# Two-step token sums in the feed-forward, and head halves joined by engine writes across partitions

## The chip, the core and the metric

The kernel runs on one core of one Trainium2 chip. The metric is the device time of one launch, in microseconds (us). The core has a matrix engine (TensorE, PE in the profile, with its weight loads as PEld), a vector engine (DVE), a scalar engine (ACT), GpSimd (POOL) and SyncE (SP), whose queue issues the DMAs. Each engine works through its own instructions in order.

## What is computed

A stack of three blocks on 512 tokens of width 1024, in float32. The first block has forget-gate attention (FOX, 8 heads of 64) and latent attention (MLA, 8 heads of 64), each with a gate. It is followed by two equal layers, each with four mixers (A: a chunkwise mLSTM, B: grouped attention, C: neighbourhood attention, D: differential attention), a gated merge, and a feed-forward part of width 2816. What the change touches is, cut from the reference:

```python
fox = _block_sweep(fq, fk, fv, ...).reshape(B, L, FOX_WIDTH) * jax.nn.silu(f_gate)
mla = _block_sweep(q, k, mv, ...).reshape(B, L, MLA_WIDTH) * jax.nn.silu(m_gate)
o = jnp.einsum('bgrqk,bkgd->bqgrd', softmax(q @ k), v)      # B; C likewise with its own keys
ffn = (jax.nn.silu(h2 @ w_ffn_gate) * (h2 @ w_ffn_up)) @ w_ffn_down
```

## The kernel before

**Precision.** Every float32 operand of a product is split into a high and a low part. A weight block is split by `split_w`: ACT writes `whi` (L221), then POOL, or DVE for every `k.lo`-th block, writes `wlo` (L223). Three matmuls follow for one product (L250 to L252). `evict_split` does the same for results in PSUM: ACT copies the high part (L211), DVE subtracts it for the low part (L212).

**What sets the order.** Only PE's order is written out by hand (`manual_schedule`). The instructions of ACT, DVE, POOL and SP are ordered at build time by the framework, with a model of time, from the order in which the code emits them and from the tile buffers that are free. A tile pool has a fixed number of buffers per tag: `t2` has 6, `yn` (`gate_tile`) has 3, `A` (the PSUM banks) has 8, `qs` and `ks` have 2.

**Heads.** FOX, MLA, B and C keep each head's output in one PSUM bank of 128 partitions by 512 tokens (`Head`). Partitions 0 to 63 hold the product with the high part of the values, 64 to 127 that with the low part, and the output is their sum. B and C run in both layers, so there are 48 heads in 24 pairs. `Head.pv` closes a head at `t == 3` by an ACT copy of the whole bank to a `t2` tile `z` (L458). For every second head `pair_out` takes a third `t2` tile `e`, has SP copy the upper half of the first head's `z` to the lower half of `e`, and the lower half of the second head's `z` to the upper half of `e`, by two DMAs (L464, L465), and has DVE add the halves that already stand on the right partitions (L466, L467). The first head of a pair thus ends in `e[0:64]`, the second in `e[64:128]`. The pair's output is then gated and split (L1027, L1073, or the `out` of B and C).

**Around a head.** `overlap` writes out PE's order map by map: scores, transposes, products with the values and the end of a head, at fixed lags, with pieces of other work (`stream`) between. DVE works meanwhile on softmax (L342, L345, L1019), on the low parts of the probabilities (L212, tile `ptl`) that the next products (L455) wait for, and on evictions of the streamed work.

**Feed-forward.** `ffn` runs once per layer. The first two gate blocks and the first two up blocks are plain (`plain`, 24 products of 512 columns each); the other 20 and 20 blocks are taken two by two in `fast_pair`, which needs 7 products of half size instead of 8. For it DVE adds and subtracts quarters of the raw weights (L599 to L602), ACT and DVE split each sum (L591, L592), and PE multiplies it with token quarters or with sums of them. `Tokens.sums` makes these four token sums once per layer, in two steps over the feature slices `c`. A step is four subtractions on DVE (L571 to L574) into four `t2` tiles, and for each a high part by ACT (L576) and a low part by DVE (L577): 8 DVE and 4 ACT instructions. The token quarters that it reads lie in two `qs` and two `cst` tiles; the two `qs` tiles are afterwards reused for weights of the fast pairs. The first sum is used by the third product of the first fast pair.

The plain part reads:

```python
gts, us = [k.silu2(plain(gw), k.t2()) for _ in range(2)], []
tok.sums()
for _ in range(2):
    us.append(plain(uw))
```

`silu2` is a tanh by ACT (L365) into a `t2` tile and a multiplication by DVE (L366). `pair` then multiplies gate and up (L1193) and splits the result (L1195, L1196).

Of the kernel before, what the change touches and what calls it, by code (L numbers as in the profile page):

```python
# [14 lines left out]
ALU = mybir.AluOpType  # L15
# [3 lines left out]
P = 128  # L19
# [146 lines left out]
def hybrid_kernel(ctx: ExitStack, tc: tile.TileContext, i: dict, out: bass.AP):  # L166
    nc = tc.nc
    V, A_, G, T_ = nc.vector, nc.scalar, nc.gpsimd, nc.tensor
# [8 lines left out]
    k = Work()  # L177
# [6 lines left out]
    def bank():  # L184
        return new(ps_, [P, 512], "A", bufs=8)

    def f(ap):
        return ap.bitcast(F32)
# [129 lines left out]
    def t2(dt=F32):  # L318
        return new(pool, [P, 512], "t2", dt, 6)
# [88 lines left out]
    class Head:  # L408

        def __init__(self, v, blocks, meta=None):
            self.v, self.blocks, self.meta, self.pt, self.pm = v, blocks, meta, {}, {}

        def trans(self, t, p, col):

# [20 lines left out]
        def pv(self, t):  # L438

            if t % 2 == 0:  # L440
                return
            if t == 1:
                self.ps = bank()
            first, second = self.blocks(t - 1), self.blocks(t)
            ph, pl = self.pt[t // 2]
            parts = [(self.meta[0], *self.pm[t // 2], 0, 256)] if self.meta else []
            for b in sorted(set(first) | set(second), key=lambda b: not (b in first and b in second)):
                lo, hi = (0 if b in first else P), (256 if b in second else P)
                parts.append((self.v(b), ph[:, b], pl[:, b], lo, hi))
            o = (t // 2) * 256  # L450
            for j, (v, ph, pl, lo, hi) in enumerate(parts):
                last = j == len(parts) - 1
                passes = [(v, ph, P), (v[:, 0:64], pl, 64)]
                for w, q, m in (passes[::-1] if last else passes):
                    T_.matmul(self.ps[0:m, o + lo:o + hi], w, q[:, lo:hi], start=(j == 0 and m == P), stop=(last and m == P))  # L455
            if t == 3:
                self.z = t2()
                A_.copy(self.z, self.ps)  # L458

    def pair_out(heads):  # L460

        a, b = (h.z for h in heads)
        e = t2()
        nc.sync.dma_start(e[0:64], a[64:128])  # L464
        nc.sync.dma_start(e[64:128], b[0:64])  # L465
        V.tensor_tensor(e[0:64], a[0:64], e[0:64], ALU.add)  # L466
        V.tensor_tensor(e[64:128], b[64:128], e[64:128], ALU.add)  # L467
        return e

    def split_y(y, hi, lo):  # L470
        A_.copy(hi, y)
# [85 lines left out]
    class Tokens:  # L557
# [5 lines left out]
        def sums(self):  # L563

            (b11, b12), (b21, b22) = self.q
            hi = new(pool, [P, 4, 4, 256], "v", F32R, 1)
            lo = [new(pool, [P, 2, 4, 256], "ks", F32R) for _ in range(2)]
            self.t = [(hi[:, j], lo[j // 2][:, j % 2]) for j in range(4)]
            for c in (slice(0, 2), slice(2, 4)):
                t = [t2().rearrange("p (k c) -> p k c", k=2) for _ in range(4)]  # L570
                V.tensor_tensor(t[0], b12[:, c], b11[:, c], ALU.subtract)  # L571
                V.tensor_tensor(t[1], b22[:, c], t[0], ALU.subtract)
                V.tensor_tensor(t[2], b22[:, c], b12[:, c], ALU.subtract)
                V.tensor_tensor(t[3], b21[:, c], t[1], ALU.subtract)  # L574
                for j in (1, 2, 0, 3):
                    A_.copy(self.t[j][0][:, c], t[j])  # L576
                    V.tensor_tensor(self.t[j][1][:, c], t[j], f(self.t[j][0][:, c]), ALU.subtract)  # L577

        def quarter(self, a, b):
            return tuple(z[:, 4 * a:4 * a + 4, 256 * b:256 * b + 256] for z in self.h)  # L580
# [90 lines left out]
    with tc.manual_schedule(engines={mybir.EngineType.PE}):  # L671
        x, spill, h = first_block(k)
        with tc.tile_pool(name="mix", bufs=1) as mix:
            k.mix = mix
            for layer in range(N_LAYERS):
                spill, h = hybrid_layer(k, spill, h, layer, layer == N_LAYERS - 1)
# [51 lines left out]
def first_body(k, fb, col, hl):  # L728
    nc, i, new, f, pool, small, bank, stream = k.nc, k.i, k.new, k.f, k.pool, k.small, k.bank, k.stream
    V, A_, G, T_ = k.V, k.A_, k.G, k.T_  # L730
    w_in, h = i["w_in"], k.tokens(hl)
# [101 lines left out]
    qw, kw, gw = (k.w_cols(i["t_" + n]) for n in ("fq", "fk", "fg"))  # L833
# [40 lines left out]
    fox = Work()  # L874
# [9 lines left out]
    mla = Work()  # L884
# [120 lines left out]
    def fox_head(hd):  # L1005
        u, e = fox.units[hd // 2], hd % 2
        st = Work()
        hobj = head(hd, *fox.v)
        fox.heads[hd] = hobj

        def sc(t):
            if t == 0:
                st.cb = new(pool, [P, L], "cb")
                nc.sync.dma_start(st.cb, fox.rows[hd].partition_broadcast(P))
            sps, n = scores(t, [(u.qs[:, e, t * P:(t + 1) * P], u.ks[:, 2 * e + b]) for b in range(2)], k.mcr)
            p = k.p_tile(n)

            r = k.softmax_of_sum([(sp, st.cb[:, a:b], a, b) for sp, a, b in sps], p)[1]
            V.tensor_scalar(p, p, r, None, ALU.mult)  # L1019
            if t == 3 and hd in (1, 3):  # L1020
                v = fox.units[hd // 2 + 2]
                v.task = stream.push(fox_unit(v), U_COST, soon=True)
            return p

        def done():
            e = k.pair_out([fox.heads[hd - 1], fox.heads[hd]])
            V.scalar_tensor_tensor(e, e, 0.5, u.gate, ALU.mult, ALU.mult)  # L1027
            y1[hd // 2] = k.y_tile()
            k.split_y(e, *y1[hd // 2])

        return [maps_of(hd, t, sc, hobj, done if t == 3 and hd % 2 else None, u) for t in range(NT)]
# [15 lines left out]
    def mla_head(hd):  # L1047
        u = mla.units[hd]
        hobj = head(hd, *mla.v)
        mla.heads[hd] = hobj  # L1050

        def sc(t):
            sl = slice(t * P, (t + 1) * P)
            (qh, ql), (kh, kl) = u.q, u.k
            sps, n = scores(t, [(qh[:, sl], kh), (qh[:, sl], kl), (ql[:, sl], kh)], k.mkr)
            p = k.p_tile(n)
            r = k.softmax_banks(sps, p)
            if t % 2:
                A_.activation(p, p, AF.Copy, bias=0.0, scale=r)
            else:  # L1060
                V.tensor_scalar(p, p, r, None, ALU.mult)
            if t == 3 and hd < 6:

                v = mla.units[hd + 2]
                v.task = stream.push(mla_unit(hd + 2, v), 1100)
                if hd % 2 == 0:
                    gate(hd // 2 + 1)
            return p

        def done():  # L1070
            j = hd // 2
            e = k.pair_out([mla.heads[hd - 1], mla.heads[hd]])
            V.scalar_tensor_tensor(e, e, 0.5, gates[j], ALU.mult, ALU.mult)  # L1073
            if j >= 2:
                q = k.q_stack()
                y2.append((q[:, 0, 0:S], q[:, 1, 0:S]))
            k.split_y(e, *y2[j])

        return [maps_of(hd, t, sc, hobj, done if t == 3 and hd % 2 else None, u, q1) for t in range(NT)]
# [68 lines left out]
def ffn(k, x, l, h, quarters, last):  # L1148
    nc, i, new, V, A_, f, pool, bank, stream = k.nc, k.i, k.new, k.V, k.A_, k.f, k.pool, k.bank, k.stream
    gw, uw = (k.w_cols(i[n][l], lambda: new(pool, [P, 2 * L], "qs")[:, 0:1024]) for n in ("t_gate", "t_up"))  # L1150
    tok = k.Tokens(h, quarters)
# [6 lines left out]
    def plain(w):  # L1158
        ps = bank()
        for _ in k.proj_t([(ps, get)], next(w), KD):  # L1160
            pass
        return ps
# [16 lines left out]
    def pair(first):  # L1179

        if first:

            k.lo = 2
            gts, us = [k.silu2(plain(gw), k.t2()) for _ in range(2)], []
            tok.sums()
            for _ in range(2):
                us.append(plain(uw))
            k.lo = 1
        else:
            gts, us = [k.silu2(g, g) for g in fast(gw)], fast(uw)  # L1190
        out = []
        for u, gt in zip(us, gts):
            V.scalar_tensor_tensor(gt, u, 0.5, gt, ALU.mult, ALU.mult)  # L1193
            hi, lo = y_tiles()
            A_.copy(hi, gt)  # L1195
            V.tensor_tensor(lo, gt, f(hi), ALU.subtract)  # L1196
            out.append((hi, lo))
        return out
# [342 lines left out]
def pair_maps(k, j, head, score, out, unit=None, before=None):  # L1541

    heads = [head(2 * j + e) for e in range(2)]

    def one(e, t):
        st = Work()

        def sc():
            st.p, st.col = score(e, t)

        def done():
            out(k.pair_out(heads))

        needs = []
        if unit and e == 0 and t == 0:
            needs.append((0, lambda: unit.task))
        if before and e == 1 and t == 3:
            needs.append((3, lambda: before))
        return (sc, lambda: heads[e].trans(t, st.p, st.col), (lambda: heads[e].pv(t)) if t % 2 else None,
                done if e == 1 and t == 3 else None, needs)  # L1560

    return [one(e, t) for e in range(2) for t in range(NT)]
# [437 lines left out]
```

## Time and profile before

| | |
|---|---|
| three runs | 2560.34, 2564.12 (median), 2567.02 us |
| the profiled execution | 2570.03 us, of it 2568.2 us from the first to the last instruction |
| PE busy | 2488.4 us (97%) |
| DVE, ACT, POOL busy | 1602.7, 1329.6, 939.0 us (62%, 52%, 37%) |
| mean granted TensorE clock | 0.99 of 2.4 GHz |
| first feed-forward, plain part and first fast pair | about 1098 to 1142 us |
| second feed-forward, the same | about 2206 to 2251 us |

PE is busy nearly throughout. Time of the other engines matters where PE waits for it, so the profile is read from PE's waits: the list of who waited for whom, and the timeline around the longest of them.

### The profile page before, as it was taken

The page shows a single profiled execution, that of the slowest core. Times are in us where ns is not written, and L with a number is a line of the kernel's source. Part 1 is how long each engine was busy: PE and PEld are TensorE (multiplying, and loading weights), DVE is VectorE, ACT ScalarE, POOL GpSimd, SP SyncE. Part 2 cuts the span into 40 slices and gives each one's busy share as a digit, 9 for nine tenths or more (in the row PEclk, how much of TensorE's full clock was granted, in tenths as well). Part 3 has the DMA queues.
Part 4 walks back from the last instruction along what each step waited for, and adds up shares of the span by engine and source line. Part 5 has one row for each costly group of instructions (what it writes and reads, how often), then busy time and mean ns, then how long its engine had stood idle before and what let it go on. Part 6 is the DMA issues. An engine that isn't in the chain of part 4 may idle for free. (4 is left out here: it accounts for less than half of the span.)

```text
span 2568.2 us, 39912 instructions
## 1 busy us (share of the span) xinstructions
PE 2488.4 (97%) x14358; PEld 2159.6 (84%) x14358; DVE 1602.7 (62%) x3521; ACT 1329.6 (52%) x2893; POOL 939.0 (37%) x834
## 2 busy tenths in 40 slices
PE   7999999999999999989999999999999999899998
PEld 7988788888888878779999888888878878799997
DVE  3577557769335354577888567584354464787886
ACT  4567646647445444354444467475354453554443
POOL 4453346542565544400000456424655534100002
PEclk9999999999999999999999999999999999999999
DMA  5552233221537332422333232214374334232232
GB/s 149 145 142 68 88 128 103 77 95 55 145 105 189 106 105 83 148 91 99 101 106 107 99 110 88 88 57 132 108 186 115 97 89 135 87 107 99 101 105 82
DMA packets 117750, 277.20 MB, mean 108 GB/s; under 512 B 15824, under 2 KB 37584, under 8 KB 117552
## 3 DMA queue, kind: packets, MB, share of 16 engines
q1 hardware_dynamic: 117552, 274.65, 35.4%
q8 instruction: 113, 1.85, 0.3%
q14 instruction: 85, 0.70, 0.1%
HBM read 230.26 MB, written 6.46 MB: 92 GB/s over the span
## 5 line engine op out<-in xcount | busy, mean ns | idle before, releaser
L223 POOL TENSOR_TENSOR wlo<-raw,whi 128x512 fp32r<-128x512 f32 (+4 forms) x481 | 617.4, 1286 | 622.9 <-ACT whi L221 598.8
L221 ACT CAST whi<-raw 128x512 fp32r<-128x512 f32 (+4 forms) x573 | 345.7, 605 | 513.5 <-PE A L251 331.8
L250 PE MATMUL A<-hi,whi 128*128 128x512 f32 (+2 forms) x1368 | 535.5, 391 | 0.7 <-ACT hi L211 0.7
L252 PE MATMUL A<-hi,wlo 128*128 128x512 f32 (+2 forms) x1368 | 515.5, 377 | 2.7 <-POOL wlo L223 2.7
L251 PE MATMUL A<-lo,whi 128*128 128x512 f32 (+2 forms) x1368 | 516.8, 378 | 0.1
L252 PEld LDWEIGHTS A<-hi,wlo 128*128 128x128 f32 x1368 | 258.4, 189 | 53.8 <-POOL wlo L223 3.5
L250 PEld LDWEIGHTS A<-hi,whi 128*128 128x128 f32 x1368 | 258.7, 189 | 37.9 <-ACT hi L211 0.8
L251 PEld LDWEIGHTS A<-lo,whi 128*128 128x128 f32 x1368 | 259.1, 189 | 37.1 <-DVE lo L212 0.3
L651 POOL TENSOR_TENSOR ptl<-raw,pth 128x512 fp32r<-128x512 f32 x20 | 26.0, 1320 | 605.7 <-ACT pth L650 605.7
L212 DVE TENSOR_TENSOR ptl<-A,pth 128x512 fp32r<-128x512 f32 (+3 forms) x256 | 148.9, 582 | 103.9 <-ACT pth L211 102.5
L316 PE MATMUL A<-ident,p 128*128 128x128 f32 (+3 forms) x1125 | 176.2, 279 | 22.9 <-DVE p L540 17.5
L250 PE MATMUL A<-v,whi 128*128 128x256 f32 x640 | 182.3, 285 | 10.7 <-ACT whi L591 10.7
L316 PEld LDWEIGHTS A<-ident,p 128*128 128x128 f32 (+3 forms) x1125 | 136.5, 140 | 62.1 <-DVE p L540 19.7
L252 PE MATMUL A<-v,wlo 128*128 128x256 f32 x640 | 181.9, 284 | 3.8 <-DVE wlo L592 3.8
L251 PE MATMUL A<-ks,whi 128*128 128x256 f32 x640 | 181.2, 283 | 0.0
L344 ACT ACTIVATE p<-p,sms 128x512 f32<-128x512 f32 (+6 forms) x160 | 100.6, 629 | 121.0 <-DVE sms L342 116.1
L211 ACT CAST pth<-A 128x512 fp32r<-128x512 f32 (+3 forms) x256 | 128.0, 500 | 65.8 <-PE A L316 64.3
L223 DVE TENSOR_TENSOR wlo<-raw,whi 128x512 fp32r<-128x512 f32 x92 | 67.0, 728 | 125.4 <-ACT whi L221 125.2
L298 PE MATMUL A<-whi,hi 128*128 128x256 f32 (+7 forms) x440 | 144.5, 328 | 0.0
L300 PE MATMUL A<-whi,lo 128*128 128x256 f32 (+7 forms) x440 | 141.7, 322 | 0.0
L299 PE MATMUL A<-wlo,hi 128*128 128x256 f32 (+7 forms) x440 | 141.6, 322 | 0.0
L250 PEld LDWEIGHTS A<-v,whi 128*128 128x128 f32 x640 | 122.4, 191 | 17.2 <-ACT whi L591 11.2
(433 smaller groups left out, 6172.7 us busy)
## 6 DMA issues: line engine op xcount, KB each, us to landing
raw<-in_t_gl_dram SPq DMA_DIRECT2D x64, 512.0 KB, 3.5
raw<-in_w_ffn_down_dram SPq DMA_DIRECT2D x44, 512.0 KB, 3.6
raw<-in_w_in_dram SPq DMA_DIRECT2D x26, 512.0 KB, 3.5
raw<-in_w_out_dram SPq DMA_DIRECT2D x24, 512.0 KB, 3.6
raw<-in_t_gate_dram SPq DMA_DIRECT2D x24, 512.0 KB, 3.6
raw<-in_t_up_dram SPq DMA_DIRECT2D x24, 512.0 KB, 3.5
qs<-in_t_gate_dram SPq DMA_DIRECT2D x20, 512.0 KB, 4.4
qs<-in_t_up_dram SPq DMA_DIRECT2D x20, 512.0 KB, 4.2
```

The source lines that it names most:

```text
L211: A_.copy(hi, ps)
L212: V.tensor_tensor(lo, ps, f(hi), ALU.subtract)
L221: A_.copy(hi, src)
L223: (V if k.lo and k.turn % k.lo == 0 else G).tensor_tensor(lo, src, f(hi), ALU.subtract)
L250: T_.matmul(ps, sh, mh, start=first, stop=False, **kw)
L251: T_.matmul(ps, sh, ml, start=False, stop=False, **kw)
L252: T_.matmul(ps, sl, mh, start=False, stop=last, **kw)
L298: T_.matmul(ps, sh, wh[:, j], start=(b + j == 0), stop=False)
L299: T_.matmul(ps, sh, wl[:, j], start=False, stop=False)
L300: T_.matmul(ps, sl, wh[:, j], start=False, stop=(b + j == nk - 1))
L316: T_.transpose(dst, src, ident[0:k, 0:k])
L344: A_.activation(dst, dst, AF.Exp, bias=st[:, e:e + 1], scale=-1.0, accum_out=st[:, 2:3])
```

## The change

- `Head` gets a `mate`, the first head of its pair (none for a first head). At `t == 3` a first head takes the tile `e`, a second head takes its mate's. ACT copies one half of the bank (64 partitions) to the other 64 partitions of `e`: 64-127 to 0-63 for a first head, 0-63 to 64-127 for a second. DVE then adds the half of the bank that stands on the right partitions, from PSUM. `pair_out`, with its two DMAs and two additions, is gone, as are the two `z` tiles.
- `Tokens.sums` becomes a generator that stops after each step. The first step is emitted behind the first plain gate block, the second behind the second. The results of these two gate blocks go to `gate_tile()` (`yn`) instead of `t2`.

```diff
@@ Head.__init__ @@
-            self.v, self.blocks, self.meta, self.pt, self.pm = v, blocks, meta, {}, {}
+            self.v, self.blocks, self.meta, self.pt, self.pm, self.mate = v, blocks, meta, {}, {}, None
@@ Head.pv @@
             if t == 3:
-                self.z = t2()
-                A_.copy(self.z, self.ps)
-
-    def pair_out(heads):
-
-        a, b = (h.z for h in heads)
-        e = t2()
-        nc.sync.dma_start(e[0:64], a[64:128])
-        nc.sync.dma_start(e[64:128], b[0:64])
-        V.tensor_tensor(e[0:64], a[0:64], e[0:64], ALU.add)
-        V.tensor_tensor(e[64:128], b[64:128], e[64:128], ALU.add)
-        return e
+                self.e = self.mate.e if self.mate else t2()
+                own, other = (slice(64, P), slice(0, 64)) if self.mate else (slice(0, 64), slice(64, P))
+                A_.copy(self.e[own], self.ps[other])
+                V.tensor_tensor(self.e[own], self.ps[own], self.e[own], ALU.add)
@@ Tokens.sums, at the end of the loop over c @@
+                yield
@@ fox_head @@
+        hobj.mate = fox.heads[hd - 1] if e else None
-            e = k.pair_out([fox.heads[hd - 1], fox.heads[hd]])
+            e = hobj.e
@@ mla_head @@
+        hobj.mate = mla.heads[hd - 1] if hd % 2 else None
-            e = k.pair_out([mla.heads[hd - 1], mla.heads[hd]])
+            e = hobj.e
@@ ffn, pair @@
-            gts, us = [k.silu2(plain(gw), k.t2()) for _ in range(2)], []
-            tok.sums()
+            gts, us, sums = [], [], tok.sums()
+            for _ in range(2):
+                gts.append(k.silu2(plain(gw), k.gate_tile()))
+                next(sums)
@@ pair_maps @@
+    heads[1].mate = heads[0]
-            out(k.pair_out(heads))
+            out(heads[1].e)
```

## Rows read from the trace of the kernel before

**Rows 1.** The page, part 1: busy time, share and instructions of each engine.
```profile
PE 2488.4 (97%) x14358; PEld 2159.6 (84%) x14358; DVE 1602.7 (62%) x3521; ACT 1329.6 (52%) x2893; POOL 939.0 (37%) x834
```

**Rows 2.** PE's waits: line, what ended them, us in total, times, longest.
```profile
PE A L250 <- ACT whi L591: 10.7, 2, 5.5
PE A L455 <- DVE ptl L212: 6.8, 4, 2.4
...
PE A L252 <- DVE wlo L592: 3.8, 2, 2.0
...
PE A L1777 <- DMA ks<-stl: 0.8, 1, 0.8
```

**Rows 3.** Timeline of PE, both feed-forwards: start, us, operation, [idle before, releaser].
```profile
1130.31 0.58 PE L250 MATMUL A<-v,whi 128*128 128x256 f32 x1 [5.25 <-ACT whi L591]
...
2239.29 0.58 PE L250 MATMUL A<-v,whi 128*128 128x256 f32 x1 [5.50 <-ACT whi L591]
```

**Rows 4.** Timeline of DVE, first feed-forward.
```profile
1106.87 0.77 DVE L223 TENSOR_TENSOR wlo<-raw,whi 128x512 fp32r<-128x512 f32 x1
1111.66 1.22 DVE L598 TENSOR_TENSOR ptl<-raw,pth 128x1024 fp32r<-128x1024 f32 x1 [4.01 <-ACT pth L597]
...
1113.40 0.68 DVE L366 SCALAR_TENSOR_TENSOR t<-t,A 128x512 f32<-128x512 f32 x1
1114.00 0.68 DVE L571 TENSOR_TENSOR t<-qs,qs 128x512 f32<-128x512 f32 x1
...
1115.99 1.79 DVE L572 TENSOR_TENSOR t<-cst,t 128x512 f32<-128x512 f32 x1
...
1128.87 0.68 DVE L600 TENSOR_TENSOR p<-p,raw 128x512 f32<-128x512 f32 x1
```

**Rows 5.** Windows at the lower clock: busy us (instructions) by engine, then granted clock, DMA.
```profile
180.30:187.13 6.83, 6.04 (x24) 4.77 (x25) 5.51 (x19) 3.48 (x9) 2.57 (x2) 0.50 0.20 58
211.00:217.83 6.83, 5.09 (x17) 4.71 (x18) 5.09 (x14) 2.11 (x7) 1.26 (x1) 0.50 0.00 0
1129.20:1136.03 6.83, 3.68 (x15) 3.38 (x16) 6.79 (x11) 2.21 (x5) 0.00 (x0) 0.50 0.23 77
2238.50:2245.33 6.83, 4.29 (x18) 3.99 (x19) 6.79 (x11) 2.55 (x5) 0.00 (x0) 0.50 0.22 80
1927.90:1931.31 3.41, 3.41 (x13) 2.73 (x11) 2.33 (x7) 2.40 (x5) 1.88 (x2) 0.50 0.09 29
```

**Rows 6.** DVE's groups by form: count, busy us, mean ns, idle before and its releaser.
```profile
L212 DVE TENSOR_TENSOR ptl<-A,pth 128x512 fp32r<-128x512 f32 x144 | 98.3, 683 | 38.4 <-ACT pth L211 37.2
...
L466 DVE TENSOR_TENSOR t<-t,t 64x512 f32<-64x512 f32 x24 | 21.2, 883 | 32.9 <-DMA t<-t 32.9
L467 DVE TENSOR_TENSOR t<-t,t 64x512 f32<-64x512 f32 x24 | 20.7, 863 | 4.4 <-DMA t<-t 3.6
...
L577 DVE TENSOR_TENSOR ks<-t,v 128x512 fp32r<-128x512 f32 x16 | 10.6, 678 | 0.0
```

**Rows 7.** Timeline of PE at four ends of head pairs.
```profile
181.09 0.58 PE L455 MATMUL A<-ptl,v 128*64 128x256 f32 x2 [2.24 <-DVE ptl L212]
...
211.31 0.46 PE L815 MATMUL A<-x,sth 96*128 96x144 f32 x1 [2.25 <-DVE v L212]
...
821.17 0.33 PE L455 MATMUL A<-ptl,v 128*64 128x256 f32 x1 [1.41 <-DVE ptl L212]
...
1927.47 0.33 PE L455 MATMUL A<-ptl,v 128*64 128x256 f32 x1 [2.37 <-DVE ptl L212]
```

**Rows 8.** Timeline of DVE at the last of these four.
```profile
1925.38 1.56 DVE L466 TENSOR_TENSOR t<-t,t 64x512 f32<-64x512 f32 x1 [0.72 <-DMA t<-t]
1926.87 0.54 DVE L212 TENSOR_TENSOR ptl<-A,pth 128x384 fp32r<-128x384 f32 x1
```

**Rows 9.** ACT's group that ends a head.
```profile
L458 ACT COPY t<-A 128x512 f32<-128x512 f32 x48 | 27.8, 579 | 20.6 <-PE A L455 20.3
```

**Rows 10.** DMA issues: count, size, median us from issue to landing.
```profile
t<-t SPq DMA_DIRECT2D x48, 128.0 KB, 3.0
```

## The prediction

> **What bounds the kernel now.** I read the page first: PE is busy 2488.4 of 2568.2 us [rows 1], so only some 80 us of idle PE can be won, and whatever is lost while PE runs below full speed. No matmul is added or removed and PE's order is written by hand, so the change can act through PE's waits and its clock alone. The list of PE's waits comes next [rows 2]. Two entries belong to the feed-forward: the wait for `whi` of L591 and the one for `wlo` of L592, twice each, once per layer, together 10.7 + 3.8 = 14.5 us. The reader should see in the timeline that the long ones fall at the third product of the first fast pair, the first to use a token sum and a sum of weights [rows 3]. There DVE is the late engine: it idles 4.01 us up to 1111.66, and from 1114.00 on it runs the token sums without a pause until L600 makes the weight sum at 1128.87 [rows 4]. PE goes on 1.44 us behind that start, at 1130.31 [rows 3]. The heads' share is in four places where PE waited 2.24 + 2.25 + 1.41 + 2.37 = 8.27 us for a low part from DVE [rows 7]. At the last one it is plain why: DVE stood 0.72 us on L466, waiting for the DMA, took 1.56 us for it, and only then made `ptl` [rows 8]; the other three show the same sequence.
>
> Last, the windows. Five stretches that begin at or behind these waits ran at a granted clock of 0.50, which is 1.2 of 2.4 GHz [rows 5]. Before each of them PE had stood idle; the wait at 821.17, 1.41 us, was followed by no fall. Work done at half clock would have taken half as long, so the price is half of PE's busy time there: (3.68 + 4.29) / 2 = 4.0 us in the feed-forwards and (6.04 + 5.09 + 3.41) / 2 = 7.3 us at the heads. At stake are thus 18.5 us in the feed-forwards and 15.6 us at the heads.
>
> **The token sums.** Nothing is added or removed. A step is 8 DVE instructions, at a spacing of 0.60 us (1113.40 to 1114.00 [rows 4]) 4.8 us, and four ACT casts. Behind the first gate block the first step can fill DVE's idle 4.01 us. It does not fit wholly: DVE also meets POOL there, and the one subtraction that met POOL before took 1.79 us for 0.68 [rows 4], 1.1 us more. That meeting lay in the stretch before L600 and moves with the step. So the stretch loses 4.8 + 1.1 us and takes up an overflow of 4.8 + 1.1 - 4.0 = 1.9 us: L600 comes 4.0 us earlier. Two things can bring it further forward. The gate results leave `t2`, so the second step no longer waits for tiles, and its first reading frees a `qs` tile for the weights of L599 earlier. DVE can then put L599 and L600 ahead of the second up block's two instructions and the like, up to four of 0.60 us. L600 would start between 1122.5 and 1124.9, PE's product could go on between 1123.9 and 1126.3, and PE was ready at 1130.31 - 5.25 = 1125.06. The first wait falls from 5.25 us to between 0 and 1.25. The second, about 2 us, stands while L592 queues behind other work, and falls where DVE is ahead. Between 0 and 3.3 us are left per layer; I take the middle, 1.7, as both ends need all of DVE's order to go one way. The gain is 14.5 - 2 x 1.7 = 11.1 us. Of the clock's 4.0 us I take 3.0, since the long idle time is gone but some remains. **Feed-forwards: 14 us**, bounds -9.6 (the step goes in front of work that PE waits for, see below; placed as before it is 0) and 18.5.
>
> What the step is moved past: `wlo` by DVE at 1106.87 [rows 4] belongs to the first up block, which begins only behind the second gate block, 24 products of 512 columns, so a few us on DVE are covered; without that cover up to the step's 4.8 us per layer would be lost. `yn` has three buffers and the gate results take two; the next user of them, `y_tiles`, comes a pair of blocks later, so I cost it at nothing. ACT's four casts lie beside the subtractions, on an engine that is half idle [rows 1]; SP is moved past nothing, it issues the two `qs` loads when the tiles come free, which is earlier.
>
> The Trainium skill, "SBUF — State Buffer", section "SBUF: two separate sides", has a rule that speaks against this part: DVE with two SBUF inputs and GpSimd share one port pair, and whoever comes second waits for the whole of the other's instruction. The trace agrees: the subtraction with two SBUF inputs was stretched to 1.79 us, while L212, which reads PSUM, averages 0.683 [rows 4, 6]. By the rule's full block a meeting would cost a POOL instruction instead of 1.1 us; that would move the sum by tenths.
>
> **The heads.** Removed are 48 DMAs of 128 KB, 3.0 us each to landing [rows 10], and 48 DVE additions, 21.2 + 20.7 us [rows 6]. The DMAs' issue time on SP is worth nothing by itself: PE's waits name a DMA once, for 0.8 us [rows 2]. Added are 48 additions on DVE. Their nearest row is L212, one input in PSUM, 0.683 us [rows 6]; half the partitions do not shorten it, as L466's 0.883 us on 64 partitions against L577's 0.678 on 128 shows. DVE's busy time falls by 41.9 - 48 x 0.683 = 9.1 us, off the path but for the places of rows 7. ACT's copy shrinks to 64 partitions and crosses them. No row shows a crossing write; I bound it by nothing and by twice L458's 0.579 us [rows 9], and take 0.58.
>
> At the four places PE then waits for its split alone. I leave 0.5 us each, below one L212, so 8.27 - 2.0 = 6.3 us come back. Of the clock's 7.3 us I take half, 3.6, since PE idles at these pipeline ends in any case; ends 0 and 7.3. Against this stands a new wait: the addition queues on DVE behind ACT's copy, now at all 48 heads instead of the 24 pairs, and softmax and the next `ptl` stand behind it. L212, the same pairing of ACT copy and DVE subtraction, waited 37.2 us in 144, 0.26 each [rows 6]: 48 x 0.26 = 12.5 us on DVE. L466 and its kind turned 32.9 us on DVE [rows 6] into 15.6 us on PE, a ratio of 0.47; but 24 of these waits replace the old ones, so I charge 24 x 0.26 x 0.47 = 2.9 us, bounds 0 and 12.5. Each bank is held about 0.7 us longer; no PE wait is put down to a bank that L458 frees, so seven other banks cover it, and without them it would be 0.7 us a head. **Heads: 6.3 + 3.6 - 2.9 = 7 us**, bounds -6 (6.3 - 12.5) and 15.6.
>
> **The sum.** 14 + 7 = 21 us against the profiled execution's 2570.0 us gives 2549.0. The median of the runs is 5.9 us (0.23%) lower, so I forecast 2564.1 - 21 = **2543 us**.
>
> **The rivals.**
> *The first step is not moved in effect.* DVE's order is made at build time by the framework, not by the code's order alone; for it: the idle 4.01 us were left although the token quarters lay ready. Against: the step now stands ahead of the next block's splits and two `t2` tiles are free. The feed-forwards then gain nothing, the heads 7: 2557 us. Chance 0.14.
> *The wait moves to the next product.* DVE is busy 6.79 of 6.83 us behind the stall [rows 5]; what is won at the third product may be lost at the fourth or at the second pair, and the clock still falls. Then some 5 us of the feed-forwards and 2 at the heads stay: 2557 us. Chance 0.12.
> *The addition's wait costs more than the DMA's did.* Place: the end of every head, DVE in order behind ACT. At w us a head PE loses 48 x 0.47 x w; it lost 15.6 us before, and the feed-forwards give 14, so it decides from w = 29.6 / 22.6 = 1.3 us on. At 2 us it loses 45, in all 2564 + 45 - 29.6 = 2580 us, slower than before. For: ACT has its own backlog, and L466 waited 32.9 / 24 = 1.4 us. Against: L212's 0.26 us. Chance 0.08.
>
> **How the numbers follow.** A measurement of this kernel can tell about 0.3%, 7.7 us, from no change. The forecast has 0.66, all of it faster. Of the first rival I count 0.05 as faster and 0.09 as the same, of the second 0.04 and 0.08, the third is slower: 0.75, 0.17, 0.08. The range goes down to 2532, where nearly all of the 34 us at stake come back, and up to 2560, which takes in both rivals at 2557; beyond are the third and a little at each end.
>
> **What would show it.** Right: in the feed-forwards DVE runs L571 to L577 before the second gate block's L366, PE's waits on L591 and L592 fall from 14.5 to 3 to 4 us, and the windows at 0.50 there vanish; no DMA `t<-t` is left, the additions take 0.68 us each, and PE's waits on L212 halve. Wrong: L600 still starts some 15 us behind the second gate's L366; new PE waits on `ptl` or `p` at head ends; or a clock that falls at as many places as before.

## The result and the profile after

| | before | after |
|---|---|---|
| median of the runs | 2564.77 us (4 runs, 2560.34 to 2567.02) | 2536.14 us (4 runs, 2534.82 to 2536.66) |
| profiled execution | 2570.03 us, span 2568.2 | 2534.82 us, span 2532.9 |
| mean granted clock | 0.99 | 0.997 |

The ratio is 0.989, 95% interval 0.9873 to 0.9907. Two further sets of runs gave 0.9876 and 0.988 (below). The kernel is 28.6 us faster between the medians, where 21 were forecast: the time lies in the range, on the fast side of the forecast.

Lines moved with the edit. The kernel after has the head's copy at L461 and its addition at L462, the products with values at L456 (L455 before), the token sums at L565 to L568 and their splits at L570 and L571 (L571 to L577), the sums of weights at L594 to L597 (L599 to L602) and their splits at L586 and L587 (L591, L592), and the gated product at L1192 to L1195 (L1193 to L1196).

The page, part 1, of the kernel after:

```profile
PE 2475.1 (98%) x14358; PEld 2149.5 (85%) x14358; DVE 1599.0 (63%) x3521; ACT 1335.2 (53%) x2893; POOL 937.3 (37%) x834
```

Against [rows 1] the span fell by 35.3 us. PE's busy time fell by 13.3 with the same 14358 instructions, which is less work at half clock, and its idle time by 22.0. DVE's and ACT's busy times hardly moved.

PE's waits in the kernel after, those that answer to [rows 2] (line, what ended them, us in total, times, longest):

```profile
PE A L252 <- DVE wlo L587: 2.1, 2, 1.1
...
PE A L250 <- DVE t L618: 1.4, 2, 0.7
...
PE A L456 <- DVE yl L212: 0.6, 1, 0.6
```

The wait on `whi` is gone, the one on `wlo` fell from 3.8 to 2.1, and a small one on L618 is new: 3.5 us in both feed-forwards instead of 14.5. No wait of the products with values on `ptl` is left (6.8 before [rows 2]), and none on the two other low parts for which PE waited at a head's end before:

```profile
PE A L815 <- DVE v L212: 2.3, 1, 2.3
...
PE A L815 <- DVE x L212: 1.0, 1, 1.0
```

Together 6.8 + 2.3 + 1.0 = 10.1 us of waits at the heads' ends are gone.

DVE's timeline in the first feed-forward of the kernel after, to be held against [rows 4] (start, us, operation, idle before and its releaser). PE's instructions are the same in both traces, so each can be compared by its start; here PE stands 14.25 us earlier than in the kernel before.

```profile
1089.53 0.69 DVE L565 TENSOR_TENSOR t<-qs,qs 128x512 f32<-128x512 f32 x1
1092.04 0.69 DVE L366 SCALAR_TENSOR_TENSOR yn<-t,A 128x512 f32<-128x512 f32 x1 [1.82 <-ACT t L365]
...
1095.14 1.78 DVE L568 TENSOR_TENSOR t<-cst,t 128x512 f32<-128x512 f32 x1
...
1098.05 0.68 DVE L565 TENSOR_TENSOR t<-qs,qs 128x512 f32<-128x512 f32 x1
...
1102.20 0.67 DVE L366 SCALAR_TENSOR_TENSOR yn<-t,A 128x512 f32<-128x512 f32 x1
...
1108.05 0.68 DVE L595 TENSOR_TENSOR p<-p,raw 128x512 f32<-128x512 f32 x1
...
1111.06 0.68 DVE L597 TENSOR_TENSOR p<-raw,p 128x512 f32<-128x512 f32 x1
1111.66 1.88 DVE L587 TENSOR_TENSOR wlo<-p,whi 128x512 fp32r<-128x512 f32 x3
```

By 1098.05 seven of the first step's eight instructions are done (ACT's cast for the eighth runs from 1097.42 to 1098.03), and the second step begins there, ahead of the second gate block's L366 at 1102.20. The idle 4.01 us are filled, and L595 (L600 before) makes its sum at 1108.05, which is 1122.3 in the time of the kernel before. PE goes on with that product at 1110.82 without a wait. What is left is L587, which stands behind L597 on DVE.

At the heads, DVE's and ACT's groups by form and DVE's timeline at the last of the four ends of [rows 7, 8]:

```profile
L462 DVE TENSOR_TENSOR t<-A,t 64x512 f32<-64x512 f32 x48 | 32.9, 686 | 35.3 <-ACT t L461 34.7
```
```profile
L461 ACT COPY t<-A 64x512 f32<-64x512 f32 x48 | 27.9, 582 | 22.9 <-PE A L456 21.8
```
```profile
1897.82 0.70 DVE L462 TENSOR_TENSOR t<-A,t 64x512 f32<-64x512 f32 x1 [1.58 <-ACT t L461]
1900.16 0.42 DVE L342 CUSTOM_DVE_ANT_0 p<-A,cb 128x256 f32<-128x256 f32 x1 [1.64 <-POOL cb L1773]
```

DVE waits 34.7 us for the copies, as long as it waited for the DMAs at L466 (32.9 [rows 6]). But behind this wait DVE idles again: nothing that PE needed stood in the queue.

The stretches of [rows 5], moved so that each takes in the same work of PE in the kernel after (same columns):

```profile
178.50:185.33 6.83, 5.22 (x35) 3.90 (x36) 6.76 (x21) 5.12 (x14) 3.96 (x4) 1.00 0.20 58
204.00:210.83 6.83, 6.60 (x49) 6.25 (x48) 6.54 (x19) 5.44 (x18) 3.80 (x6) 1.00 0.22 77
1108.30:1115.13 6.83, 5.76 (x47) 5.37 (x46) 6.83 (x12) 4.38 (x8) 0.00 (x0) 1.00 0.29 79
2203.20:2210.03 6.83, 5.77 (x47) 5.37 (x46) 6.83 (x12) 4.68 (x9) 0.00 (x0) 1.00 0.22 79
1902.00:1905.41 3.41, 3.41 (x22) 2.94 (x21) 2.60 (x7) 1.24 (x3) 3.41 (x4) 1.00 0.28 92
```

All five run at 1.00, 2.4 GHz: in the third, 47 matmuls where [rows 5] had 15 in the same time. Of the ten falls to 0.50 before the kernel's last few us, three are left (two and three in the two repeats below).

### The profile page after: what moved, and what is told of

Same layout as the page of the kernel before. It is cut to its first block, busy times and chain, and to the rows that moved or that the text cites. A ratio compares the mean times of both kernels' runs of the same rounds, so it can differ in the third digit from the quotient of the medians.

```text
span 2532.9 us, 39802 instructions
## 1 busy us (share of the span) xinstructions
PE 2475.1 (98%) x14358; PEld 2149.5 (85%) x14358; DVE 1599.0 (63%) x3521; ACT 1335.2 (53%) x2893; POOL 937.3 (37%) x834
## 3 DMA queue, kind: packets, MB, share of 16 engines
q1 hardware_dynamic: 113712, 268.36, 34.7%
## 5 line engine op out<-in xcount | busy, mean ns | idle before, releaser
L586 ACT CAST whi<-p 128x512 fp32r<-128x512 f32 x160 | 99.0, 622 | 64.7 <-PE A L251 58.8
```

## The experiments

All ratios are to the kernel before, run on the same chip in the same set.

| kernel | median, us | ratio, 95% interval | span, us |
|---|---|---|---|
| set 1: before | 2571.41 | | |
| sums only | 2552.34 | 0.9935, 0.9921 to 0.9948 | 2550.6 |
| heads only | 2552.91 | 0.9934, 0.9922 to 0.9947 | 2552.5 |
| crossing by ACT from SBUF | 2543.3 | 0.9899, 0.9885 to 0.9913 | 2542.0 |
| DMA, addition from PSUM | 2552.46 | 0.9932, 0.9917 to 0.9947 | 2554.4 |
| set 2: before | 2567.67 | | |
| after, again | 2536.11 | 0.9876, 0.9858 to 0.9893 | 2534.2 |
| gates in `t2` | 2541.49 | 0.9896, 0.9878 to 0.9915 | 2538.2 |
| sums at once, gates in `yn` | 2552.58 | 0.9939, 0.9923 to 0.9955 | 2548.8 |
| eight more on DVE | 2550.85 | 0.9931, 0.9912 to 0.995 | 2549.5 |
| set 3: before | 2567.87 | | |
| after, a third time | 2538.04 | 0.988, 0.9865 to 0.9895 | 2535.8 |
| copy twice | 2541.87 | 0.9895, 0.9877 to 0.9912 | 2539.3 |
| copy four times | 2559.93 | 0.9966, 0.9952 to 0.998 | 2558.2 |
| two low parts on POOL | 2542.25 | 0.9897, 0.9882 to 0.9912 | 2540.8 |

### Each part alone

The kernel before with the edits of `Tokens.sums` and `pair` alone:

```diff
+                yield
...
-            gts, us = [k.silu2(plain(gw), k.t2()) for _ in range(2)], []
-            tok.sums()
+            gts, us, sums = [], [], tok.sums()
+            for _ in range(2):
+                gts.append(k.silu2(plain(gw), k.gate_tile()))
+                next(sums)
```

> The kernel before with the sums in two steps and the gate results in the yn tiles; the heads still end with the DMAs. Theory (the two parts add up, each by PE's waits and by the falls of the clock behind them): the two feed-forwards are some 14 us shorter, the windows at 0.50 behind the first fast pair are gone, the heads keep their waits behind L466; about 2551 us, ratio 0.9945. Rival (the parts help each other, since a fall of the clock or the planned order in one place carries over to the other): under 7 us gained here, 2558 us or more.

The kernel after with that part undone, so that it has the change of the heads alone:

```diff
-                yield
...
-            gts, us, sums = [], [], tok.sums()
-            for _ in range(2):
-                gts.append(k.silu2(plain(gw), k.gate_tile()))
-                next(sums)
+            gts, us = [k.silu2(plain(gw), k.t2()) for _ in range(2)], []
+            tok.sums()
```

> The kernel after with the sums formed at once behind both gate blocks and the gate results in t2, as before; the heads are joined by engine writes. Theory (parts add up): what the whole change gained (28.6 us between the medians) less the 14 us of the feed-forwards, so about 2550 us, ratio 0.9943; the two long waits of 5 us at the first fast pair and the two windows at 0.50 behind them are there, the falls at the heads are not. Rival of the prediction's size (heads worth 7 us): 2557 us. If the new wait of DVE on ACT (34.7 us in the trace after) cost what the wait on the DMA cost, 2565 us.

PE's waits with the sums only, then with the heads only:

```profile
PE A L455 <- DVE ptl L212: 6.1, 4, 2.3
...
PE A L252 <- DVE wlo L593: 2.1, 2, 1.1
```
```profile
PE A L250 <- ACT whi L585: 10.6, 2, 5.4
...
PE A L252 <- DVE wlo L586: 4.3, 3, 2.0
```

Each part removes its own waits and leaves the other's. By the ratios the sums are worth 0.65% of 2567 us, 16.7 (13.4 to 20.3), and the heads 0.66%, 16.9 (13.6 to 20.0); 0.9935 x 0.9934 = 0.987, which is the whole change within its intervals. By the starts of PE's instructions in the feed-forwards, the sums gain 6.7 and 7.0 us there. The span with the heads alone is 15.7 us shorter than before; PE's busy time is 2477.7, so 10.7 of these are clock and 5.0 idle time.

### What held the heads: the DMA or the addition

The crossing is kept off the DMAs but no longer rides on the eviction: ACT copies the whole bank, then two halves across partitions in SBUF, and DVE adds as before.

```diff
...
+                self.z = t2()
+                A_.copy(self.z, self.ps)
+                if self.mate:
+                    a, b = self.mate.z, self.z
+                    e = self.e = t2()
+                    A_.copy(e[0:64], a[64:128])
+                    A_.copy(e[64:128], b[0:64])
+                    V.tensor_tensor(e[0:64], a[0:64], e[0:64], ALU.add)
+                    V.tensor_tensor(e[64:128], b[64:128], e[64:128], ALU.add)
```

> The kernel after, but each head is copied whole to SBUF by ACT as before, and at the pair's end two ACT copies cross the halves from SBUF to SBUF and two DVE additions with two SBUF inputs join them: no DMA, but the additions may again be stretched beside POOL, and ACT has 48 copies more. Theory (the heads' gain comes from the DMA that DVE, in order, stood on): most of the heads' gain stays, 2536 to 2542 us, no window at 0.50 at the heads. Rival (the gain comes from the addition reading PSUM, which POOL cannot hold up): most of the heads' gain is lost, about 2548 us, and the additions average near 0.87 us.

The opposite: DVE's new addition from PSUM is kept, and the half crosses by DMA.

```diff
-                A_.copy(self.e[own], self.ps[other])
+                z = t2()
+                A_.copy(z[other], self.ps[other])
+                nc.sync.dma_start(self.e[own], z[other])
```

> The kernel after, but the crossing half goes through an SBUF tile and a DMA, per head, and the addition reads PSUM as after. Theory (the DMA that DVE stands on): the heads' gain is lost, 2550 us or more, with DVE's wait on the DMA at 33 us or more and falls of the clock at head ends. Rival (the stretched additions): the gain stays, 2536 to 2540 us, additions at 0.69 us.

With ACT crossing from SBUF, DVE's groups by form and PE's wait for a low part:

```profile
L467 DVE TENSOR_TENSOR t<-t,t 64x512 f32<-64x512 f32 x24 | 23.6, 982 | 2.8 <-ACT t L465 2.1
L466 DVE TENSOR_TENSOR t<-t,t 64x512 f32<-64x512 f32 x24 | 18.0, 749 | 25.6 <-ACT t L464 25.4
```
```profile
PE A L456 <- DVE ptl L212: 3.7, 2, 2.2
```

With the DMA, ACT's copy and DVE's addition, DVE's timeline at a head's end, and PE's waits:

```profile
L462 ACT COPY t<-A 64x512 f32<-64x512 f32 x48 | 27.8, 579 | 18.7 <-PE A L456 18.0
```
```profile
L464 DVE TENSOR_TENSOR t<-A,t 64x512 f32<-64x512 f32 x48 | 33.0, 688 | 68.6 <-DMA t<-t 66.2 <-ACT pth L211 2.2
```
```profile
174.64 0.68 DVE L464 TENSOR_TENSOR t<-A,t 64x512 f32<-64x512 f32 x1 [2.20 <-DMA t<-t]
175.24 0.54 DVE L212 TENSOR_TENSOR ptl<-A,pth 128x384 fp32r<-128x384 f32 x1
```
```profile
PE A L456 <- DVE ptl L212: 4.9, 6, 1.8
...
PE A L316 <- DVE p L1017: 2.8, 2, 2.4
```

The addition takes 0.69 us in either kernel, but with the DMA in front of it DVE waits 66.2 us, PE waits again behind DVE, and the heads' whole gain is lost (0.9932 is the sums' alone). With ACT from SBUF, 2543.3 us, most of it stays, though DVE and ACT do more than before. So the DMA's time to landing was the price, not DVE's additions. What the changed kernel has beyond that is smaller: additions of 0.686 us instead of 0.749 and 0.982, 48 copies fewer on ACT, and the 3.7 us of waits that come back here.

### The order of the sums, or the freed tiles

The changed kernel, in two variants: the gate results back in `t2`; and the gate results in `yn`, with both steps behind the second gate block.

```diff
-                gts.append(k.silu2(plain(gw), k.gate_tile()))
+                gts.append(k.silu2(plain(gw), k.t2()))
```

> The kernel after, but the results of the two plain gate blocks stay in t2. By the step of the prediction that the gates' leaving t2 frees the second step: the second step's first subtraction goes behind the second gate's L366 again, L595 starts later by 1 to 2.4 us per layer, and PE's waits at the first fast pair grow by as much: 2 to 5 us more than the kernel after. Rival (the yn tiles do nothing, DVE's idle 4.01 us alone count): no difference, within 1 us.

```diff
-            gts, us, sums = [], [], tok.sums()
-            for _ in range(2):
-                gts.append(k.silu2(plain(gw), k.gate_tile()))
-                next(sums)
+            gts, us = [k.silu2(plain(gw), k.gate_tile()) for _ in range(2)], []
+            list(tok.sums())
```

> The kernel after, but both steps are formed behind both gate blocks, with the gate results in yn. Theory (DVE's idle time before the second gate is filled only by a step that is emitted in front of it): the gain of the feed-forwards is lost, 12 to 14 us more than the kernel after, with the waits of 5 us at the first fast pair. Rival (the order in the code does not matter to the framework, the free t2 tiles let the sums come early): no difference from the kernel after.

The changed kernel itself ran beside them:

> The kernel after, unchanged, beside the next three on one chip, to set their sizes against it. Theory (the parts add up, 0.55% + 0.65%): ratio 0.988 to 0.990 as on the first chip. If the two parts hinder each other, 0.991 or more; the sum of the two alone on the second chip would be 0.987.

DVE's timeline of the kernel with the sums at once, then PE's waits there:

```profile
1098.35 1.23 DVE L593 TENSOR_TENSOR ptl<-raw,pth 128x1024 fp32r<-128x1024 f32 x1 [3.51 <-ACT pth L592]
...
1114.69 0.67 DVE L595 TENSOR_TENSOR p<-p,raw 128x512 f32<-128x512 f32 x1
```
```profile
PE A L250 <- ACT whi L586: 9.0, 2, 4.5
...
PE A L252 <- DVE wlo L587: 4.7, 3, 2.3
```

Freed tiles without the order give back nothing that can be told: the idle stretch of [rows 4] is there again (3.51 us), the sum of L595 comes at 1114.69, the waits are 13.7 us of the 14.5 before, and the kernel is 16.5 us slower than the changed one between the medians, 14.6 between the spans, where 12 to 14 were expected. The order without the freed tiles keeps most: 5.4 us slower between the medians, with intervals that overlap, and 4.0 between the spans. In its trace some 2 us of these lie in the feed-forwards, with one fall of the clock at 2212.30; L565 starts there only at 1093.81, behind the first gate's L366, where the changed kernel has it ahead, and the second step's L565 at 1102.77, behind the second gate's L366, as expected.

### Eight more instructions on DVE in the second step

```diff
             for c in (slice(0, 2), slice(2, 4)):
...
+                for _ in range(8 if c.start else 0):
+                    V.tensor_tensor(t[0], t[0], t[0], ALU.max)
```

> The kernel after with eight more DVE instructions of 128x512 (the maximum of a tile with itself) in the chain of the second step, once per layer: at least 4.8 us on DVE in front of L595. Theory (waits and the fall of the clock behind them): PE's waits at the first fast pair grow from 1.75 to about 6.5 us per layer and a window at 0.50 follows in each layer, which costs 1.8 to 2.1 us more: 13 to 14 us more than the kernel after. Rival (the clock's fall has another cause than PE's idle time): 9.6 us more and no window at 0.50 there.

ACT's timeline in the first feed-forward of this kernel, and PE's wait:

```profile
1116.64 1.34 ACT L572 CAST v<-t 128x512 fp32r<-128x512 f32 x2 [3.95 <-DVE t L567]
1117.89 0.37 ACT L612 COPY t<-A 128x256 f32<-128x256 f32 x1
```
```profile
PE A L250 <- ACT t L612: 14.0, 2, 7.1
```

Eight instructions at the spacing of 0.60 us are 4.8 us of DVE per layer. PE's waits grew from 3.5 to 14.0 us, 5.2 per layer: at this place DVE's time reaches PE whole. With two falls of the clock the kernel lost 14.7 us. The way is a new one, though. DVE's sums of weights were early; the cast of the token sum (L572) was late on ACT, and L612, which empties the bank that PE's next product takes, stood behind it in ACT's queue.

### How long the heads' addition may wait

```diff
                 A_.copy(self.e[own], self.ps[other])
+                for _ in range(1):
+                    A_.copy(self.e[own], self.ps[other])
```

The second kernel repeats it three times.

> ACT writes the same crossing copy twice, so every one of the 48 additions can start 0.58 us later, 28 us of added waiting on DVE at most. Theory (DVE's wait behind the copy is slack: in the changed kernel it waits 34.7 us there and no wait of PE stands behind it): within 4 us of the changed kernel, and what is lost shows at the ends of the four head pipelines alone. Rival (the prediction's charge: 0.47 us on PE for each us that DVE waits): 48 x 0.58 x 0.47 = 13 us slower than the changed kernel. The additions themselves stay at 0.69 us.

> ACT writes the crossing copy four times, so every addition can start 1.74 us later, above the 1.3 us a head from which the third rival of the prediction makes the kernel slower than before. Theory (slack): the loss stays far below the prediction's rate; at the four ends, where PE needs the next split, up to 4 x 1.74 = 7 us and a fall of the clock or two, 2 to 10 us slower than the changed kernel, still faster than before. Rival (0.47 us on PE for each us on DVE): 48 x 1.74 x 0.47 = 39 us slower than the changed kernel, about 11 us slower than before. ACT is also busier by 84 us; if its other casts come late behind the copies, new waits of PE on ACT tiles show that.

> The changed kernel itself, unaltered, as the baseline for the two edits run beside it. Its ratio to the kernel before stood at 0.989 and 0.988 in two sets of runs; 0.988 to 0.989 is expected again, with no fall of the clock in the feed-forwards and 1.75 us of PE's waits left in each.

DVE's addition with the copy made twice, then four times:

```profile
L464 DVE TENSOR_TENSOR t<-A,t 64x512 f32<-64x512 f32 x48 | 33.0, 687 | 39.9 <-ACT t L463 39.3
```
```profile
L464 DVE TENSOR_TENSOR t<-A,t 64x512 f32<-64x512 f32 x48 | 33.0, 687 | 48.0 <-ACT t L463 47.2
```

The copy twice costs 3.8 us, with intervals that overlap, within the 4 that were expected and below the 13 of the prediction's charge. Four times costs 21.9 us, which neither side had: far more than 10, far less than 39. But DVE waited only 4.6 and 12.5 us longer than in the changed kernel, not 28 and 84, which fits an order made at build time that puts other work in front of a late addition. For waits of that length the rate of 0.47 asks 2.2 and 5.9 us, so these two kernels do not decide between slack and that rate. Of the 22.4 us between the spans 16.6 were lost between 170 and 370 us, where FOX ends and MLA runs, and twice as many falls of the clock came with it (six, not three). Of PE's waits in this kernel (sums over the whole of it) these fall there in the main, one of them on ACT (3.1 us in the changed kernel):

```profile
PE A L316 <- ACT p L1058: 4.5, 2, 3.0
...
PE A L316 <- DVE p L1017: 1.2, 2, 0.9
PE A L812 <- DVE x L212: 1.2, 1, 1.2
PE A L298 <- DVE ptl L212: 1.0, 1, 1.0
```

Elsewhere PE has two more waits on ACT, which the changed kernel does not have:

```profile
PE A L1695 <- ACT p L334: 2.8, 4, 1.0
...
PE A L250 <- ACT p L334: 1.3, 2, 0.6
```

ACT is busy 81.5 us more in this kernel, and PE's waits on ACT grew by some 6 us; how the rest of the loss divides between DVE's wait and ACT's queue stays open. What it does show is that a head's end has room for about one copy more, not for three. The kernel is still 7.9 us faster than before, but the token sums are in that figure: with the sums only the ratio was 0.9935, here it is 0.9966, so with four copies the heads' change costs more than it gains.

### Two low parts on POOL

An attempt at the 1.75 us per layer that are left:

```diff
-                    V.tensor_tensor(self.t[j][1][:, c], t[j], f(self.t[j][0][:, c]), ALU.subtract)
+                    (G if j in (0, 3) else V).tensor_tensor(self.t[j][1][:, c], t[j], f(self.t[j][0][:, c]), ALU.subtract)
```

> The changed kernel with the low parts of the first and the fourth token sum made by POOL: DVE loses four instructions of 0.68 us per layer from the stretch ahead of the first fast pair. Theory (DVE's order is what is left of the feed-forward's stall): the 1.75 us of PE's waits left per layer go, 2 to 4 us faster than the changed kernel. Rival (POOL's two-input subtraction from SBUF takes 1.66 us and stretches DVE's instruction beside it, as L568 was stretched to 1.78 us): each of the four meets DVE and costs it 1.1 us, which gives back all of the 0.68 us saved; no faster, or up to 4 us slower.

POOL's timeline in the first feed-forward, DVE's beside it, and PE's new wait:

```profile
1092.01 1.40 POOL L571 TENSOR_TENSOR ks<-t,v 128x512 fp32r<-128x512 f32 x1 [0.30 <-ACT v L570]
1093.51 1.60 POOL L223 TENSOR_TENSOR wlo<-raw,whi 128x512 fp32r<-128x512 f32 x1
1097.06 1.56 POOL L571 TENSOR_TENSOR ks<-t,v 128x512 fp32r<-128x512 f32 x1 [1.95 <-ACT v L570]
```
```profile
1092.18 1.78 DVE L567 TENSOR_TENSOR t<-cst,qs 128x512 f32<-128x512 f32 x1
1093.88 1.78 DVE L223 TENSOR_TENSOR wlo<-raw,whi 128x512 fp32r<-128x512 f32 x1
...
1097.39 1.78 DVE L565 TENSOR_TENSOR t<-qs,qs 128x512 f32<-128x512 f32 x1
```
```profile
1104.36 0.50 PE L252 MATMUL A<-hi,wlo 128*128 128x512 f32 x1 [2.63 <-DVE wlo L223]
```

The rival held. Six of POOL's seven instructions from 1090 to 1108 us meet a DVE instruction, which ends 0.55 us behind POOL's end (1092.01 + 1.40 = 1093.41; 1092.18 + 1.78 = 1093.96) instead of taking 0.68 us. DVE saves 0.60 us, its spacing, per instruction handed over and loses 1.1 per meeting; the next `wlo` of the plain part comes late, PE waits 2.63 us for it, and the kernel is 4.2 us slower than the changed one, with intervals that overlap. By the rule of the Trainium skill, "SBUF — State Buffer", section "SBUF: two separate sides", the second of the two waits for the whole rest of the first's instruction; the trace agrees, to 0.01 us in these three meetings. No version that was run beats the changed kernel.

## Why the prediction was right, and where not

**The bound.** As forecast, nothing acts but PE's waits and its clock: of the 35.3 us between the spans 22.0 are idle time and 13.3 clock.

**The token sums: right, term by term.** L600 was to start between 1122.5 and 1124.9; it starts at 1122.3, 0.2 us ahead of that. Left per layer were to be 1.7 us; 1.75 are (1.07 and 0.7). The waits gave 11.0 us for 11.1. By PE's starts the two feed-forwards gained 6.64 and 7.04, 13.7 together, so 2.7 was clock, for 3.0. The sum of 14 stands in the traces; the ratio of the sums alone gives 16.7, with 14 inside the interval. The meeting with POOL came along, 1.78 us, as charged. Off was only a detail, the overflow of 1.9 us. The second gate's L366 starts 3.05 us later than before (1102.20 + 14.25 against 1113.40), of which 1.8 are three subtractions of the second step, so some 1.3 us of the first step overflowed; its first subtraction had found room ahead of the first gate's L366. Of the parts of this edit the order is worth nearly everything and the free `t2` tiles at most the 5.4 us of the kernel without them. The cover named for the plain part's `wlo` on DVE is real and limited: nothing shows in the changed kernel, and in the kernel with POOL's low parts, where DVE comes to its second `wlo` 4.4 us later (1103.62 against 1100.39, in a trace that stands 1.17 us earlier), PE waits 2.63 us for it.

**The heads: the mechanism was right, the term undersized: 7 forecast, 16.9 (13.6 to 20.0) by the ratio of the heads alone.** Three numbers made it.

- The clock's half, 3.6. Half may have been too little: the long idle times at the pipeline ends went, and all three windows of [rows 5] at the heads went with them, in the changed kernel and with the heads alone, which by the prediction's reckoning is the whole 7.3. But which falls an execution has varies. Two further falls are missing in each of the two kernels, and not the same two (576.2 and 1678.7 us of the kernel before with the heads alone, 1883.5 and 2078.1 in the changed kernel); the kernel with the sums only, whose heads are the old ones, lacks those at 180.3, 1678.7 and 1883.5; and the profiled execution of before stood 5.9 us above its median. From before to the heads alone PE's busy time fell by 10.7 us, from the sums only (2479.9) to the changed kernel, the same step, by 4.8. So the clock's share is not known more closely than this.
- The charge for the new wait, 2.9. The wait itself came larger than forecast, 34.7 us and 0.72 a head instead of 0.26. At 0.47 us on PE per us on DVE that would be 16 us, and no wait of PE is put down to it (0.9 us in each of the two repeats). This rate, taken from the DMA's waits, was the error. It came from a wait that had PE's next low part right behind it [rows 8]; the addition now follows the last product by a copy of 0.58 us, where a copy and 3.0 us of DMA lay between, and at the place shown above DVE had nothing else to do before or behind it. The kernel with four copies shows that this room is limited.
- The 6.3 of waits. 10.1 came back: the prediction left 0.5 us at each of its four places, 2.0 in all, and passed over two shorter waits on low parts (0.98 us at 212.74, 0.83 at 292.26); with the heads alone and in the changed kernel nothing is left at any of the six. PE's idle time fell by only 5.0 us with the heads alone, as other small waits differ from kernel to kernel: those for DMAs are 4.8 us there, 0.8 before and 2.9 in the changed kernel.

With 10.1 of waits, no charge and 3.6 to 7.3 of clock the term would have been 13.7 to 17.4, inside the interval of the heads alone.

**The rivals.** The first step was moved in effect; the sums at once show what the first rival would have been, 16.5 us slower than the changed kernel between the medians. The wait did not move on but for 0.7 us at L618. The third rival's place is real, its rate is not: 0.72 us a head were to cost 16 us and left no wait of PE in the profile. Its limit of 1.3 us a head was not reached: with four copies DVE waits 47.2 / 48 = 0.98 us a head, and what that kernel loses has ACT's queue in it.

## What to carry to other kernels

Where the matrix engine is nearly always busy, look for the late engine's idle stretch in front of its overload: eight instructions that were ready earlier, moved there, were worth all of their time, and the clock's falls went with the stalls. A transfer between partitions through a DMA costs its time to landing on the chain from the last product to the joined tile; an engine that evicts anyway can write across partitions for nothing. A wait of a helper engine is priced by what stands behind it in its queue, not by its length.

## What the runs showed that was not expected

- ACT's copy of 64 partitions onto the other 64 takes 0.582 us, the copy of all 128 in place took 0.579 [rows 9]: crossing costs nothing, and half the partitions save nothing. The kernel with the DMA copies 64 partitions in place, in 0.579 us, so neither hides the other.
- DVE's 34.7 us of waiting at the heads, as long as the 32.9 for the DMAs, left no wait on PE in the profile of the kernel after (in its two repeats one of 0.9 us).
- A DVE instruction with two SBUF inputs that meets POOL ends 0.55 us behind POOL's end, whatever its own start: it runs after POOL, not beside it at a lower rate. In the changed kernel 64 of 66 such meetings of 128x512 instructions ended 0.50 to 0.60 us behind POOL's end, though DVE started 0.03 to 1.45 us behind POOL's start.
